# Full-height instead of half-height products with the low parts of the keys, in forgetting attention

## The chip, the cores and the metric

The kernel runs on one core of a Trainium2 chip. The metric is device microseconds from start to end of one execution; the number given for a kernel is the median of several executions.

## What is computed

Two transformer blocks follow each other on 1,024 tokens of width 1,024, in fp32. The second block holds a sliding-window attention and a *forgetting attention* of 8 heads of width 64. The change touches the latter alone:

```python
s = jnp.einsum('bhqd,bhsd->bhqs', qb, kh).astype(jnp.float32) * scale
s = s + cq[..., None] - c_k[:, :, None, :]
s = jnp.where((k_pos[None, :] <= q_pos[:, None])[None, None], s, -jnp.inf)
probs = jax.nn.softmax(s, axis=-1)
return jnp.einsum('bhqs,bhsd->bhqd', probs.astype(vh.dtype), vh)
```

## The kernel before

TensorE multiplies in fp32r, a form that is less exact than fp32. So every operand is split into a high part (a copy rounded to fp32r, made by ScalarE) and a low part (what is left, subtracted by VectorE or GpSimd), and a product is made of several terms that add up in one PSUM bank. A dense layer (`mm3`, line 160) takes three terms for each of eight 128-row blocks: high by high, low by high, and high by the weights' low part, 24 matmuls of 512 columns for a half of the tokens. `dense` (line 170) runs this for one block of 128 output features and calls `then` with each half's PSUM bank; there are three such banks (`mm=3`, line 34).

Forgetting attention works on pairs of heads, j = 0 to 3. A pair's queries and keys come from one dense layer each.

- `queries` (line 1142) makes, for each head e of the pair, a tile of 128 partitions. The 64 partitions of the head's own place hold the high part of the scaled query, the other 64 hold its low part.
- `keys` (line 1159) makes for each head a tile `kh[e]` in which the key's high part stands twice, in the own 64 partitions and in the other 64 (line 1170, ScalarE). Its low part, `kl`, is subtracted on VectorE (line 1172). The sliding-window attention calls it with `twice` true: two tiles `kl[e]`, each with the low part in both halves of the partitions. Forgetting attention calls it with `twice` false: one tile `kl[0]` for both heads, each head's low part in its own 64 partitions.
- `fox_scores` (line 1261) goes over blocks of 128 queries (i = 0 to 7, two for each g), both heads, and pieces of at most 512 keys. A piece is two matmuls into one PSUM bank, of which the tag `sc` has two. Line 1281 multiplies all 128 partitions of the query tile with `kh[e]`, which gives (high + low) by high. Line 1282 multiplies the 64 partitions with the query's high part by the 64 partitions of `kl[0]`, which gives high by low. VectorE then adds the forgetting bias and takes the row's maximum (line 1289), ScalarE takes the exponential (line 1299), GpSimd divides by the sum (line 1304). `fox_pv` (line 1308) transposes the result on TensorE (line 1320), splits it (`split`, line 144) and multiplies it with the values (line 1327).
- `swa_block` (line 1199), the sliding-window counterpart, has the same two terms with full-height tiles in both matmuls (lines 1210 and 1211).

`run` (line 1335) writes the program in this order: scores of a group g, then the values' product of the group before it, then one dense layer of the output gates as work in between (`filler`). After g = 2 it makes the next pair's queries, keys and bias rows. The last pair (j = 3) has no next pair; its `filler` calls find nothing left, and only the first products of the next stage (`after`) can go between.

In this part of the kernel the order on each engine is not written by hand: the compiler's scheduler orders the instructions by a simulated timeline, with the program order as priority. Each engine then runs its own list strictly in that order. The tiles `kh`, `kl`, the bias rows and the values come from a pool with the tag `q`, opened at line 1646 with 10 buffers of 4 KB in each partition.

Of the kernel before, what the change touches and what calls it, by code (L numbers as in the profile page):

```python
# [11 lines left out]
F32R = mybir.dt.float32r  # L12
I32 = mybir.dt.int32
AF = mybir.ActivationFunctionType
ALU = mybir.AluOpType
# [303 lines left out]
def run(thread):  # L319

    while True:
        try:
            next(thread)
        except StopIteration as e:
            return e.value
# [32 lines left out]
def hs(hf):  # L358
    return slice(H * hf, H * hf + H)
# [702 lines left out]
class Attention:  # L1062
# [93 lines left out]
        yield from k.dense(self.w["w_in2"], m, self.xn, then)  # L1156
        return s

    def keys(self, m, twice):

        k = self.k
        nc = k.nc
        kh = [k.q("kh", F32R) for _ in range(2)]
        kl = [k.q("kl", F32R) for _ in range(2 if twice else 1)]

        def then(hf, ps):
            for e in range(2):
                own, other = slice(64 * e, 64 * e + 64), slice(64 - 64 * e, 128 - 64 * e)
                for o in (own, other):
                    nc.scalar.copy(out=kh[e][o, hs(hf)], in_=ps[own])  # L1170
                for o in (own, other) if twice else (own,):
                    nc.vector.tensor_tensor(
                        out=kl[e if twice else 0][o, hs(hf)], in0=ps[own], in1=kh[e][own, hs(hf)], op=ALU.subtract)

        yield from k.dense(self.w["w_in2"], m, self.xn, then)
        return kh, kl
# [84 lines left out]
    def fox_scores(self, st, g):  # L1261
        k = self.k
        nc = k.nc
        qs, kh, kl, cs = st
        out = {}
        for i in (2 * g, 2 * g + 1):

            rest = k.t("S2", tag="tp") if 4 <= i < 6 else None
            for e in range(2):
                own = slice(64 * e, 64 * e + 64)  # L1270
                qc = slice(128 * i, 128 * i + 128)
                diag = k.a("cd", [128, 128])
                nc.vector.tensor_tensor(out=diag, in0=cs[e][:, qc], in1=self.cmsk, op=ALU.add)
                pieces = []
                mx = None
                for c0 in range(0, 128 * i + 128, H):
                    n = min(H, 128 * i + 128 - c0)
                    kc = slice(c0, c0 + n)
                    s = rest[:, 256 * e:256 * e + n] if c0 and rest is not None else k.t("S", tag="tp")[:, :n]
                    ps = k.ps("sc", name="pss")[:, :n]  # L1280
                    nc.tensor.matmul(ps, lhsT=qs[:, e, qc], rhs=kh[e][:, kc], start=True, stop=False)  # L1281
                    nc.tensor.matmul(ps, lhsT=qs[own, e, qc], rhs=kl[0][own, kc], start=False, stop=True)  # L1282
                    d = min(n, 128 * i - c0)
                    parts = [(0, d, cs[e][:, c0:c0 + d])] if d > 0 else []
                    if d < n:
                        parts.append((d, n, diag))
                    for a, b, bias in parts:
                        m2 = self.small()
                        nc.vector.tensor_tensor_reduce(
                            out=s[:, a:b], in0=ps[:, a:b], in1=bias, scale=1.0,  # L1290
                            scalar=NEG if mx is None else mx, op0=ALU.add, op1=ALU.max, accum_out=m2)
                        mx = m2
                    pieces.append(s)
                nm = self.small()
                nc.vector.tensor_scalar(out=nm, in0=mx, scalar1=-1.0, scalar2=None, op0=ALU.mult)
                sums = []
                for s in pieces:
                    sums.append(self.small())
                    nc.scalar.activation(out=s, in_=s, func=AF.Exp, bias=nm, accum_out=sums[-1])
                if len(sums) == 2:  # L1300
                    nc.vector.tensor_tensor(out=sums[0], in0=sums[0], in1=sums[1], op=ALU.add)
                nc.vector.reciprocal(sums[0], sums[0])  # L1302
                for s in pieces:
                    nc.gpsimd.tensor_scalar(out=s, in0=s, scalar1=sums[0], scalar2=None, op0=ALU.mult)  # L1304
                out[i, e] = pieces
        return out
# [28 lines left out]
    def run(self, after):  # L1335
        gates = list(range(16))

        def filler(n=1):
            for _ in range(n):
                if gates:  # L1340
                    run(self.gate(gates.pop(0), (1,)))

        run(self.forget())
        kh, kl = run(self.keys(4, True))
        v = run(self.values(5))
        pend = None
        for kv in range(2):
            bias = self.swa_bias(kv)
            qs = [run(self.queries(2 * kv + b)) for b in range(2)]
            for i in range(8):  # L1350
                sc = self.swa_block(kv, i, qs, kh, kl, v, bias)
                if pend is not None:
                    self.swa_pv(*pend)
                pend = (kv, i, v, *sc)
                if i in GSWA:
                    filler()
        self.swa_pv(*pend)
        pend = None
        q, (kh, kl), cs, v = run(self.queries(6)), run(self.keys(10, False)), self.fox_bias(0), None
        for j in range(4):  # L1360
            nxt = None
            for g in range(4):
                sc = self.fox_scores((q, kh, kl, cs), g)
                if pend is not None:
                    self.fox_pv(*pend)
                if g == 0:
                    v = run(self.values(14 + j))
                pend = (j, v, g, sc)
                if g == 2 and j < 3:
                    nxt = run(self.queries(7 + j)), run(self.keys(11 + j, False)), self.fox_bias(j + 1)  # L1370
                elif (j, g) == (3, 2):
                    filler(16)
                    after = after()
                elif (j, g) == (3, 3):
                    next(after)
                else:
                    filler()
            if nxt is not None:
                q, (kh, kl), cs = nxt
        self.fox_pv(*pend)  # L1380
# [91 lines left out]
def tile_blocks(ctx, tc, a, out):  # L1472
    k = Kernel(ctx, tc, a["vec"])
    nc = k.nc
# [140 lines left out]
    def ffn(ff, x, first, n):  # L1615

        k.a.open("quad", QUAD, "right")
        q = Quads(k)
        q.operands(x)
        run(ff.ups(range(first), x, (1,)))  # L1620
        run(ff.quads(range(first, n), q))
        k.a.close("quad")
        ff.alloc()
        k.a.open("att", ATT, "right")
        for ci in range(len(ff.chunks) - 1):
            run(ff.downs(ci))
# [16 lines left out]
    k.split_engine = nc.gpsimd  # L1643
    ff1.finish(finish1, lambda: att.gates(0, range(16)))
    k.a.close("acc")
    k.a.open("q", dict(q=10))
    br = Branches(k, a, sw_d, fx_d, gt_d, h2_d, h3_d)

    def after():
# [114 lines left out]
```

## Time and profile before

| | before |
|---|---|
| median of 3 runs | 3093.22 us |
| lowest and highest run | 3089.76 and 3104.17 us |
| the profiled execution | 3081.66 us |
| its span, first to last instruction | 3079.9 us |
| mean granted TensorE clock | 0.971 of full speed |

The profile is of one execution, whose time lies 11.56 us under the median. Times inside it are counted from the first instruction. PE is TensorE's matmul, PEld its weight load, DVE is VectorE, ACT is ScalarE, POOL is GpSimd. Forgetting attention runs from about 1778 us to 2115 us, behind the sliding-window attention.

### The profile page before, as it was taken

The page shows a single profiled execution, that of the slowest core. Times are in us where ns is not written, and L with a number is a line of the kernel's source. Part 1 is how long each engine was busy: PE and PEld are TensorE (multiplying, and loading weights), DVE is VectorE, ACT ScalarE, POOL GpSimd, SP SyncE. Part 2 cuts the span into 40 slices and gives each one's busy share as a digit, 9 for nine tenths or more (in the row PEclk, how much of TensorE's full clock was granted, in tenths as well). Part 3 has the DMA queues.
Part 4 walks back from the last instruction along what each step waited for, and adds up shares of the span by engine and source line. Part 5 has one row for each costly group of instructions (what it writes and reads, how often), then busy time and mean ns, then how long its engine had stood idle before and what let it go on. Part 6 is the DMA issues. An engine that isn't in the chain of part 4 may idle for free.

```text
span 3079.9 us, 39432 instructions
## 1 busy us (share of the span) xinstructions
PE 2911.5 (95%) x14392; PEld 2318.3 (75%) x14392; DVE 1813.9 (59%) x3228; ACT 1262.6 (41%) x2187; POOL 1011.8 (33%) x1056
## 2 busy tenths in 40 slices
PE   7969899998998999999999999999998999999997
PEld 5747677777777777788778877777887887888886
DVE  6635555447886666344646755576756444444477
ACT  5434333234544444322445655564334443222233
POOL 2153333421445443003643445550026541000343
PEclk8989899899999999999999999999999999999999
DMA  6533433225422222423542221216533333533224
GB/s 210 183 107 115 117 87 88 76 72 165 153 93 82 82 71 95 150 62 113 175 131 74 83 64 65 66 52 229 178 123 111 122 110 129 186 103 103 89 89 137
DMA packets 188194, 349.72 MB, mean 114 GB/s; under 512 B 58712, under 2 KB 69464, under 8 KB 188000
## 3 DMA queue, kind: packets, MB, share of 16 engines
q1 hardware_dynamic: 146368, 268.51, 28.6%
q10 hardware_dynamic: 41632, 78.69, 7.0%
q8 instruction: 113, 1.85, 0.3%
q14 instruction: 81, 0.66, 0.1%
HBM read 265.05 MB, written 82.08 MB: 113 GB/s over the span
## 4 chain that ended last, share of the span: by engine, by line
PE 62%; DVE 5%; DMA 2%; issue 2%; ACT 1%; POOL 1%; ACTq 0%; DVEq 0%; SPq 0%; POOLq 0%
PE ps_mm L165 38%; PE psX L935 10%; PE psZ L935 5%; PE psY L935 2%; PE pso L1327 1%; PE pss L1282 1%; PE pst L1320 1%; DVE sq L255 1%; PE pss L1281 1%; POOL s L921 1%; PE pso L1243 0%; DVE wl L146 0%; DVE T L907 0%; PE pst L1238 0%; DVE g L1450 0%
## 5 line engine op out<-in xcount | busy, mean ns | idle before, releaser
L145 ACT CAST wh<-wr 128x1024 fp32r<-128x1024 f32 (+2 forms) x343 | 318.2, 928 | 651.8 <-PE ps_mm L165 532.5
L165 PE MATMUL ps_mm<-xh,wh 128*128 128x512 f32 x1344 | 546.5, 407 | 3.5 <-ACT xh L145 1.7
L165 PE MATMUL ps_mm<-xl,wh 128*128 128x512 f32 x1344 | 543.5, 405 | 1.8 <-DVE xl L146 1.8
L146 POOL TENSOR_TENSOR wl<-wr,wh 128x1024 fp32r<-128x1024 f32 (+1 forms) x109 | 257.0, 2359 | 846.5 <-ACT wh L145 663.2
L165 PE MATMUL ps_mm<-xh,wl 128*128 128x512 f32 x1344 | 369.2, 405 | 0.0
L165 PE MATMUL ps_mm<-hh,wh 128*128 128x512 f32 x864 | 342.9, 397 | 7.8 <-DVE acc L1029 4.0
L165 PE MATMUL ps_mm<-hl,wh 128*128 128x512 f32 x864 | 342.6, 397 | 0.0
L146 DVE TENSOR_TENSOR wl<-wr,wh 128x1024 fp32r<-128x1024 f32 (+2 forms) x234 | 251.7, 1076 | 105.2 <-PE ps_mm L165 51.4
L165 PEld LDWEIGHTS ps_mm<-xh,wh 128*128 128x128 f32 x1344 | 256.9, 191 | 61.6 <-issue 3.2
L165 PEld LDWEIGHTS ps_mm<-xl,wh 128*128 128x128 f32 x1344 | 256.9, 191 | 57.4 <-DVE xl L146 2.3
L165 PEld LDWEIGHTS ps_mm<-xh,wl 128*128 128x128 f32 x1344 | 249.7, 191 | 55.2 <-issue 1.9
L1029 DVE TENSOR_TENSOR acc<-acc,ps_mm 128x512 f32<-128x512 f32 x176 | 120.8, 687 | 247.4 <-PE ps_mm L165 239.5
L165 PE MATMUL ps_mm<-hh,wl 128*128 128x512 f32 x864 | 234.1, 397 | 0.0
L165 PEld LDWEIGHTS ps_mm<-hh,wh 128*128 128x128 f32 x864 | 163.7, 189 | 47.3 <-DVE acc L1029 4.4
L677 POOL TENSOR_TENSOR pr<-mt,lt 128x60 f32<-128x60 f32 (+24 forms) x248 | 88.2, 356 | 321.6 <-DMA lt<-d_l 302.8
L165 PEld LDWEIGHTS ps_mm<-hh,wl 128*128 128x128 f32 x864 | 163.7, 190 | 38.2
L165 PEld LDWEIGHTS ps_mm<-hl,wh 128*128 128x128 f32 x864 | 163.8, 190 | 38.0
L921 POOL TENSOR_TENSOR s<-wr 128x512 f32<-128x512 f32 x60 | 88.1, 1468 | 272.4 <-DMA wr<-in_w_up 149.2
L1304 POOL TENSOR_SCALAR S<-S,sm 128x512 f32<-128x512 f32 (+3 forms) x96 | 119.1, 1251 | 94.2 <-DVE sm L1302 65.8
L904 POOL TENSOR_TENSOR r<-xh,xl 128x512 f32<-128x512 f32 x32 | 70.9, 2243 | 227.9 <-PE ps_mm L165 109.6
L255 DVE TENSOR_TENSOR sq<-sq 128x512 f32<-128x512 f32 x112 | 120.8, 1078 | 35.3 <-ACT sq L253 23.1
L805 DVE SCALAR_TENSOR_TENSOR ft<-c,vec,ft 128x1023 f32<-128x1023 f32 x68 | 92.0, 1352 | 40.7 <-ACT ft L803 40.6
(379 smaller groups left out, 5852.3 us busy)
## 6 DMA issues: line engine op xcount, KB each, us to landing
wr<-in_w_in SPq DMA_DIRECT2D x58, 512.0 KB, 4.0
wr<-in_w_up SPq DMA_DIRECT2D x54, 512.0 KB, 3.5
h<-hid SPq DMA_DIRECT2D x108, 256.0 KB, 4.2
wr<-in_w_ff SPq DMA_DIRECT2D x54, 512.0 KB, 3.6
wr<-in_w_in2g SPq DMA_DIRECT2D x32, 512.0 KB, 3.6
hid<-c ACTq DMA_DIRECT2D x26, 512.0 KB, 2.9
wr<-in_w_ff SPq DMA_DIRECT2D x48, 256.0 KB, 2.7
hid<-ft ACTq DMA_DIRECT2D x17, 512.0 KB, 2.6
```

The costliest lines, as they stand in the source:

```text
L145: self.nc.scalar.copy(out=pair[0], in_=src)
L146: (engine or self.nc.vector).tensor_tensor(out=pair[1], in0=src, in1=pair[0], op=ALU.subtract)
L165: self.nc.tensor.matmul(ps, lhsT=a[:, j, :cols], rhs=x[j][hf][part], start=i == 0, stop=i == 3 * kb - 1)
L255: self.nc.vector.tensor_tensor(out=sq, in0=acc, in1=sq, op=ALU.add)
L677: e.tensor_tensor(out=pr, in0=mt[:, :n, i:i + 1].to_broadcast([128, n, m]), in1=lt[:, i:i + 1, i + 1:].to_broadcast([128, n, m]), op=ALU.mult)
L805: nc.vector.scalar_tensor_tensor(out=t[:, i:], in0=src[:, :-i], scalar=c(2 - i), in1=t[:, i:], op0=ALU.mult, op1=ALU.add)
L904: nc.gpsimd.tensor_tensor(out=raw[n], in0=pr[0], in1=pr[1], op=ALU.add)
L921: nc.gpsimd.tensor_tensor(out=o, in0=x, in1=y, op=op)
L935: self.k.nc.tensor.matmul(ps, lhsT=a[:, j], rhs=x[j][part], start=start and i == 0, stop=i == 3 * half - 1, skip_group_check=True)
L1029: k.nc.vector.tensor_tensor(out=o, in0=o, in1=ps, op=ALU.add)
L1281: nc.tensor.matmul(ps, lhsT=qs[:, e, qc], rhs=kh[e][:, kc], start=True, stop=False)
L1304: nc.gpsimd.tensor_scalar(out=s, in0=s, scalar1=sums[0], scalar2=None, op0=ALU.mult)
```

## The change

`keys` always makes two tiles of low parts, each with the low part in both halves of the partitions, as the sliding-window attention had them already. The second matmul of a piece takes all 128 partitions of the query tile and of `kl[e]`, so it gives (high + low) by low, which adds the term low by low. VectorE has two more subtractions in each half of each of the four keys' layers. The pool of tag `q` gets 12 buffers in place of 10.

```diff
-    def keys(self, m, twice):
+    def keys(self, m):
...
         kh = [k.q("kh", F32R) for _ in range(2)]
-        kl = [k.q("kl", F32R) for _ in range(2 if twice else 1)]
+        kl = [k.q("kl", F32R) for _ in range(2)]
...
                 for o in (own, other):
                     nc.scalar.copy(out=kh[e][o, hs(hf)], in_=ps[own])
-                for o in (own, other) if twice else (own,):
+                for o in (own, other):
                     nc.vector.tensor_tensor(
-                        out=kl[e if twice else 0][o, hs(hf)], in0=ps[own], in1=kh[e][own, hs(hf)], op=ALU.subtract)
+                        out=kl[e][o, hs(hf)], in0=ps[own], in1=kh[e][own, hs(hf)], op=ALU.subtract)
...
-                own = slice(64 * e, 64 * e + 64)
...
                     nc.tensor.matmul(ps, lhsT=qs[:, e, qc], rhs=kh[e][:, kc], start=True, stop=False)
-                    nc.tensor.matmul(ps, lhsT=qs[own, e, qc], rhs=kl[0][own, kc], start=False, stop=True)
+                    nc.tensor.matmul(ps, lhsT=qs[:, e, qc], rhs=kl[e][:, kc], start=False, stop=True)
...
-    k.a.open("q", dict(q=10))
+    k.a.open("q", dict(q=12))
```

The calls in `run` lose the second argument of `keys`; nothing else changes there.

## Rows read from the trace of the kernel before

**Rows 1.** The page, busy time of each engine, share of the span, instructions

```profile
PE 2911.5 (95%) x14392; PEld 2318.3 (75%) x14392; DVE 1813.9 (59%) x3228; ACT 1262.6 (41%) x2187; POOL 1011.8 (33%) x1056
```

**Rows 2.** Windows: length, busy PE, PEld, DVE, ACT, POOL, granted clock, DMA

```profile
1648.00:1778.00 130.00, 129.33 (x729) 111.29 (x728) 99.19 (x285) 82.57 (x223) 56.77 (x44) 1.00 0.30 87
...
1778.00:2020.00 242.00, 242.00 (x1167) 185.64 (x1166) 140.51 (x460) 127.86 (x279) 122.17 (x85) 1.00 0.21 64
2020.00:2115.00 95.00, 89.68 (x464) 67.57 (x463) 72.62 (x222) 55.24 (x125) 45.83 (x34) 0.98 0.37 121
```

**Rows 3.** Windows, line 1282 alone: length, busy PE, PEld (instructions), clock, DMA

```profile
1778.00:1850.00 72.00, 8.10 (x19) 3.47 (x19) 1.00 0.21 61
1850.00:1925.00 75.00, 9.07 (x21) 3.84 (x21) 1.00 0.19 64
1925.00:2020.00 95.00, 11.94 (x27) 4.94 (x27) 1.00 0.22 66
2020.00:2080.00 60.00, 13.17 (x29) 5.40 (x29) 0.97 0.17 51
```

**Rows 4.** Waits of VectorE, 1778 to 2020 us: total us, times, longest

```profile
DVE S L1289 <- PE pss L1282: 49.1, 34, 3.0
```

**Rows 5.** Timeline around one piece of 512 keys: start, length, instruction, [idle before]

```profile
1888.40 0.40 PE L165 MATMUL ps_mm<-xl,wh 128*128 128x512 f32 x1
...
1888.64 0.40 PE L165 MATMUL ps_mm<-xh,wl 128*128 128x512 f32 x1
1888.64 0.19 PEld L1281 LDWEIGHTS pss<-kh,qs 128*128 128x128 f32 x1
1888.87 0.39 PE L1281 MATMUL pss<-kh,qs 128*128 128x512 f32 x1
...
1889.19 0.18 PEld L1282 LDWEIGHTS pss<-kl,qs 64*128 64x128 f32 x1 [0.36 <-issue]
1889.19 0.50 PE L1282 MATMUL pss<-kl,qs 64*128 64x512 f32 x1
...
1889.62 0.19 PEld L1327 LDWEIGHTS pso<-pTh,vl 128*128 128x128 f32 x1 [0.24 <-issue]
1889.62 0.39 PE L1327 MATMUL pso<-pTh,vl 128*128 128x256 f32 x1
```

**Rows 6.** Timeline, two pieces in direct succession, 512 and 128 keys

```profile
1893.08 0.40 PE L1281 MATMUL pss<-kh,qs 128*128 128x512 f32 x1
...
1893.40 0.50 PE L1282 MATMUL pss<-kl,qs 64*128 64x512 f32 x1
...
1893.83 0.33 PE L1281 MATMUL pss<-kh,qs 128*128 128x128 f32 x1
...
1894.09 0.32 PE L1282 MATMUL pss<-kl,qs 64*128 64x128 f32 x1
...
1894.35 0.38 PE L1327 MATMUL pso<-pTh,vl 128*128 128x256 f32 x1
```

**Rows 7.** Timeline, sliding-window attention: the same pair of terms, full height, 256 keys

```profile
1736.15 0.28 PE L1210 MATMUL pss<-kh,qs 128*128 128x256 f32 x1
1736.15 0.19 PEld L1211 LDWEIGHTS pss<-kl,qs 128*128 128x128 f32 x1
1736.27 0.28 PE L1211 MATMUL pss<-kl,qs 128*128 128x256 f32 x1
1736.27 0.19 PEld L1210 LDWEIGHTS pss<-kh,qs 128*128 128x128 f32 x1
1736.38 0.28 PE L1210 MATMUL pss<-kh,qs 128*128 128x256 f32 x1
```

**Rows 8.** Instructions on tile kl: count, ns min/median/max, first and last start, forms

```profile
L1282 PE MATMUL pss<-kl,qs x96: 322/490/686, 1778.6 to 2074.1; 64*128 64x512 f32 x48, 64*128 64x128 f32 x16, 64*128 64x256 f32 x16, 64*128 64x384 f32 x16
...
L1172 DVE TENSOR_TENSOR kl<-ps_mm,kh x24: 678/689/696, 1612.3 to 2016.3; 64x512 fp32r<-64x512 f32 x24
```

More of the change, by code (lines that the diff above doesn't have):

```diff
@@ L1343, in run @@
         run(self.forget())
-        kh, kl = run(self.keys(4, True))
+        kh, kl = run(self.keys(4))
         v = run(self.values(5))
@@ L1358, in run @@
         pend = None
-        q, (kh, kl), cs, v = run(self.queries(6)), run(self.keys(10, False)), self.fox_bias(0), None
+        q, (kh, kl), cs, v = run(self.queries(6)), run(self.keys(10)), self.fox_bias(0), None
         for j in range(4):
@@ L1369, in run @@
                 if g == 2 and j < 3:
-                    nxt = run(self.queries(7 + j)), run(self.keys(11 + j, False)), self.fox_bias(j + 1)
+                    nxt = run(self.queries(7 + j)), run(self.keys(11 + j)), self.fox_bias(j + 1)
                 elif (j, g) == (3, 2):
```

## The prediction

> **What bounds the kernel now.** I began with the page: TensorE (PE) is busy 95% of the span, VectorE 59% [rows 1]. That is an average, so I cut the span into stages. In the stretch 1778 to 2020 us, the first three pairs of heads, PE is busy 242.00 us of 242.00 at a granted clock of 1.00, its 2.4 GHz level; VectorE has 58%, ScalarE 53%, GpSimd 50% [rows 2]. The view of waits lists none at all for PE there, while VectorE waits 49.1 us for line 1282's products [rows 4]. So here every microsecond that PE's list becomes shorter should come off the time. In 2020 to 2115 us, the last pair and what follows, PE is busy 89.68 us of 95 and VectorE 76% [rows 2]: PE sometimes runs dry, and time saved on it may turn into waiting.
>
> A busy PE is not a PE at its best pace, since matmuls overlap. What counts is the time from one start to the next. Two dense matmuls of 512 columns start 0.24 us apart, and the next start comes 0.23 us later [rows 5]. A piece of the scores behaves differently. Line 1281 starts at 1888.87, line 1282 at 1889.19, the next matmul at 1889.62: 0.32 and 0.43 us in place of 0.23 twice. The weight loads show why. Line 1281's load starts at 1888.64, while the dense matmul before it streams. Line 1282's load, half height, waits: PEld idles 0.36 us and the load starts together with its own matmul's record, at 1889.19. The next load is full height again and starts only at 1889.62, after 0.24 us of idling [rows 5]. Both changes of height cost; nobody else is waited for ("issue").
>
> The sliding-window attention gives the comparison: the same pair of terms into the same kind of bank, but full height in both. Its load for line 1211 starts at 1736.15, beside line 1210's matmul, and 256-column matmuls start 0.12, 0.11 us apart [rows 7].
>
> **The change part by part.** *The taller matmul.* Time goes by columns, and these stay. The rows of the sliding window are what the changed code will issue, so I expect its pace: 0.23 us for 512 columns, 0.117 for 256. A lone piece of 512 then takes 0.46 us in place of 0.75 and saves 0.29. In direct succession the wide piece takes 0.75 too, and the 128-column piece behind it 0.26 + 0.26 = 0.52 [rows 6]. Two ordinary 128-column matmuls are between 0.12 us (a quarter of 0.46, by columns) and 0.23 (the pace of 256 columns, if the load sets it): it saves 0.29 to 0.40. So a piece saves at least 0.29 us. I take 0.31, because most pieces stand between other work, and 0.34, the mean of 0.29 and 0.40, as upper bound.
>
> There are 96 pieces, 48 of 512, 16 each of 384, 256 and 128 columns [rows 8]. 19 + 21 + 27 = 67 of them start before 2020 us and 29 after [rows 3]. The 67 lie where PE never waits: 67 x 0.31 = 20.8 us, all on the path. The 29 are worth 29 x 0.31 = 9.0 us on PE. Both ends are possible, nothing and all of it; PE is still busy 94% there but leaves 5.3 us idle although no piece was short, so a shorter list will partly end in the wait behind it. What is late next is the chain VectorE (line 1289), ScalarE (1299), GpSimd (1304), then the transposes. I take half, 4.5 us.
>
> *The added subtractions.* `then` runs twice in each of four keys' layers and gets two more operations each time: 16 x 0.689 us = 11.0 us on VectorE [rows 8], all ahead of 2020 us. Cost on the path between 0 and 11.0 us. VectorE rises from 140.5 to 151.5 us in a stretch that shrinks to about 221 us, 68%, still under the 76% at which PE was seen to run dry [rows 2]. The cover is the dense work in PE's list. Queued behind the new operations on VectorE are line 1289's evictions, which free the two score banks, and the probability splits. The new operations also hold the keys' dense bank 1.4 us longer; with three banks of 24 matmuls x 0.23 = 5.5 us each, PE comes back to it 11 us later. I take a fifth, 2.2 us, nearer to nothing since PE shows no wait there.
>
> *The pool.* A pair holds 8 buffers after the change (before 7): two each of kh, kl, bias rows and values. The next pair's keys take 4 (before 3). 8 + 4 = 12 and 7 + 3 = 10, so both fill the pool exactly, and the bias rows wait for a release as now. No DMA is added or moved. In the sliding window two more buffers can hold scores, but PE is busy 129.33 us of 130 there [rows 2], so I give that nothing (at most 0.7 us).
>
> *Sum:* 20.8 + 4.5 - 2.2 = 23.1 us. Against the profiled execution this makes 3081.66 - 23.1 = 3058.6 us. That execution is 11.56 us under the median of the runs, so I carry the difference over: 3093.22 - 23.1 = 3070.1 us.
>
> **The rivals.** *A, VectorE takes over.* The scheduler lays out every engine's list anew, with longer VectorE work at each hand-over of keys. If PE then waits for evictions in half of the 67 pieces, the last 29 give nothing and 2 us of the subtractions show, 10.4 - 2 = 8 us are left: 3085 us. For it: VectorE at 68% is not far from 76%, and new lists can leave PE without dense work in between. Against it: VectorE waits 49.1 us for the very products that come earlier [rows 4].
>
> *B, the change doesn't do what it says:* the pause belongs to something else, say to the second term's load from the same query tile, and stays. Then nothing is saved and the subtractions are hidden: 3093 us. Against it stand the sliding window's pairs, which have all that and no pause [rows 7]. The Trainium skill, "TensorEngine Tiling (Array Packing)", section Key Properties, says that a change of the tiling mode drains TensorE; the two idle times of 0.36 and 0.24 us agree, and the page gives no price.
>
> *C, slower:* a full-height load can't run beside a full-height matmul, and today's half-height load is what is cheap. Its place would be both loads of each of the 96 pieces; its price 0.19 us for each load [rows 5], so a piece of 512 takes 2 x (0.23 + 0.19) = 0.84 us in place of 0.75, 96 x 0.09 = 8.6 us more. With the subtractions partly in the open, by 0 to 11.0 us, the time is 3102 to 3113 us. It decides as soon as loads are no longer started under the matmul before them. The rows speak against it: the 128-row load of line 1281 runs under a 128-row dense matmul, and line 1211's under line 1210's [rows 5, 7]. The Trainium skill, "TensorE: Matmul & The Clock Gate", Part 3, The mechanism, says that a load overlaps with matmuls in flight only where their row groups differ, which would be this rival; the trace disagrees, with the load of 0.19 us at 1736.15 under the 0.28 us matmul of the same rows [rows 7].
>
> **How the numbers follow.** The forecast has 0.70, A 0.18, B 0.07, C 0.05. What a measurement of this kernel can tell from no change is about 0.5%, 15.5 us. The forecast's own span: at the low end all 96 pieces at 0.34, 32.6 us, with 3060.6; two more microseconds for the scatter of the runs, 3058. At its high end 67 x 0.29 = 19.4 us less half of the subtractions, 5.5, is 13.9 us, 3079. The range has to take in A as well, so it goes on to 3086 and leaves out B and C, 0.12, and a little beyond. Faster by over 0.5%: nearly all of the forecast and the better end of A, 0.71. Within 0.5%: most of A, all of B, 0.24. Slower: C, 0.05.
>
> **What would show it.** In the changed profile the loads of lines 1281 and 1282 should start under the matmul before them, without idling, and a lone 512-key piece should take 0.46 us from line 1281's start to the start of the next matmul. Line 1172 has 40 instructions in place of 24, 32 of them in the four pairs. The stretch with the first 67 pieces should be some 19 us shorter, with PE still showing nearly no waits; the last 29 should bring between 0 and 9 us, with more PE waits on lines 1289 and 146. The prediction is wrong if the pace of the pieces stays at 0.75 us (B), if it rises (C), or if PE's waits in the first three pairs come to more than some 10 us (A).

## The result, and the profile after

The changed kernel takes 3063.91 us (median, 3051.18 to 3067.94), beside 3094.70 us of the kernel before in the same series: 30.8 us less, a ratio of 0.9889 with a 95% interval of 0.986 to 0.9918. With more runs (below) it is 0.9904, 0.9889 to 0.992. I had forecast 3070.1 us, 23.1 us less, in a range of 3058 to 3086.

The page of the changed kernel, busy time of each engine, against [rows 1]:

```profile
PE 2883.5 (94%) x14392; PEld 2316.4 (76%) x14392; DVE 1822.0 (59%) x3244; ACT 1260.5 (41%) x2187; POOL 1003.5 (33%) x1056
```

As many matmuls, 28.0 us less of PE, and 16 more operations on VectorE. Line numbers behind 1270 are one lower now: 1280 and 1281 are the two products of a piece.

The timeline of the changed kernel around one piece of 512 keys, against [rows 5]:

```profile
1886.02 0.39 PE L165 MATMUL ps_mm<-xh,wh 128*128 128x512 f32 x1
1886.02 0.19 PEld L1280 LDWEIGHTS pss<-kh,qs 128*128 128x128 f32 x1
1886.25 0.40 PE L1280 MATMUL pss<-kh,qs 128*128 128x512 f32 x1
1886.25 0.19 PEld L1281 LDWEIGHTS pss<-kl,qs 128*128 128x128 f32 x1
1886.48 0.39 PE L1281 MATMUL pss<-kl,qs 128*128 128x512 f32 x1
1886.49 0.19 PEld L165 LDWEIGHTS ps_mm<-xl,wh 128*128 128x128 f32 x1
1886.71 0.40 PE L165 MATMUL ps_mm<-xl,wh 128*128 128x512 f32 x1
```

Every load starts under the matmul ahead of it, none idles first, and the piece takes 0.46 us from line 1280's start to the next matmul's, where it took 0.75.

Now the stages. Windows cut at the first score, the 67th piece and the last product with the values; first the kernel before, then the changed one (length; busy PE, PEld, DVE, ACT, POOL; granted clock; DMA):

```profile
1778.20:2018.00 239.80, 239.80 (x1158) 183.98 (x1156) 139.41 (x455) 127.06 (x277) 121.50 (x84) 1.00 0.21 64
2018.00:2102.80 84.80, 80.02 (x422) 59.91 (x422) 63.99 (x214) 51.03 (x120) 45.17 (x34) 0.98 0.31 100
```

```profile
1789.00:2005.50 216.50, 216.23 (x1159) 183.52 (x1158) 147.82 (x467) 125.65 (x274) 121.95 (x84) 1.00 0.22 69
2005.50:2087.00 81.50, 71.95 (x422) 57.47 (x421) 64.73 (x219) 51.42 (x121) 44.98 (x34) 1.00 0.33 109
```

The stretch of the first 67 pieces is 23.3 us shorter and PE is still busy nearly all of it. VectorE is at 68% there. The last stretch is 3.3 us shorter, PE idles 9.6 us in it in place of 4.8, and VectorE is at 79%. Together 26.6 us. What VectorE waited for the second product fell from the 49.1 us of [rows 4]; this is the changed kernel's view of its waits:

```profile
DVE S L1288 <- PE pss L1281: 24.1, 22, 2.4
```

The two profiled executions, 3081.66 and 3067.94 us, differ by 13.7 us only, because the stages ahead, whose code is the same, took longer in the second. The first product of the sliding-window attention shows it, in the view of the tile pss (count, ns, first and last start), before and after:

```profile
L1210 PE MATMUL pss<-kh,qs x64: 222/281/384, 1648.2 to 1767.3; 128*128 128x256 f32 x56, 128*128 128x128 f32 x8
```

```profile
L1210 PE MATMUL pss<-kh,qs x64: 222/281/383, 1659.2 to 1778.2; 128*128 128x256 f32 x56, 128*128 128x128 f32 x8
```

It starts 11.0 us later. Executions differ by several microseconds there whatever the change (the two profiles of the kernel before have 1648.2 and 1656.5 us), so I read what the change did from stretches that begin behind this point, and from medians.

### The profile page after: what moved, and what is told of

The parts are those of the page before. It is cut to its first block, busy times and chain, and to the rows that moved or that the text cites. A ratio compares the mean times of both kernels' runs of the same rounds, so it can differ in the third digit from the quotient of the medians.

```text
span 3066.2 us, 39452 instructions
## 1 busy us (share of the span) xinstructions
PE 2883.5 (94%) x14392; PEld 2316.4 (76%) x14392; DVE 1822.0 (59%) x3244; ACT 1260.5 (41%) x2187; POOL 1003.5 (33%) x1056
## 4 chain that ended last, share of the span: by engine, by line
PE 59%; DVE 6%; POOL 2%; issue 2%; DMA 2%; ACT 2%; ACTq 0%; SPq 0%; DVEq 0%; POOLq 0%
PE ps_mm L165 39%; PE psX L935 9%; PE psZ L935 5%; PE psY L935 2%; POOL s L921 1%; DVE sq L255 1%; PE pso L1326 1%; PE pst L1319 1%; DMA wr<-in_w_ff 1%; PE pso L1243 0%; PE pss L1280 0%; PE pss L1281 0%; DVE T L907 0%; DVE wl L146 0%; PE pst L1238 0%
## 5 line engine op out<-in xcount | busy, mean ns | idle before, releaser
L677 POOL TENSOR_TENSOR pr<-mt,lt 128x60 f32<-128x60 f32 (+24 forms) x248 | 96.9, 391 | 328.7 <-DMA lt<-d_l 309.9
```

What stands on the lines that cost most here:

```text
L677: e.tensor_tensor(out=pr, in0=mt[:, :n, i:i + 1].to_broadcast([128, n, m]), in1=lt[:, i:i + 1, i + 1:].to_broadcast([128, n, m]), op=ALU.mult)
```

## The experiments

The theory: each change between full and half height makes TensorE pause, the change takes two of them out of each of 96 pieces, and the added subtractions and buffers are hidden. Rivals: the larger pool brings part of the gain; the subtractions cost some of it; the pause belongs to something else than the height.

**The changed kernel again**, without an edit.

> The changed kernel once more, with more runs, to narrow its gain. Its trace shows the stretch from the first score to the last of forgetting attention about 27 us shorter, while the stage ahead of it (unchanged code) was 11 us longer than in the profile of before. If the change does nothing outside this stretch, the ratio settles at 0.990 to 0.992 (25 to 31 us less). If something else in it helps (the larger pool, other lists for the engines), it stays near 0.989 or goes below.

3061.90 us, ratio 0.9904 (0.9889 to 0.992), so 25 to 34 us less. Its profile has 216.40 us for the first 67 pieces and 81.60 for the rest, as the first one had. The ratio came to the place that the stretch alone explains, though its interval also takes in 0.989.

```profile
1781.00:1997.40 216.40, 216.13 (x1158) 183.44 (x1157) 147.75 (x466) 125.50 (x274) 121.68 (x84) 1.00 0.23 69
1997.40:2079.00 81.60, 72.70 (x422) 58.69 (x422) 64.79 (x219) 51.27 (x121) 45.14 (x34) 0.98 0.34 109
```

**The tall product alone.**

```diff
# before
-                    nc.tensor.matmul(ps, lhsT=qs[own, e, qc], rhs=kl[0][own, kc], start=False, stop=True)
+                    nc.tensor.matmul(ps, lhsT=qs[:, e, qc], rhs=kl[0][:, kc], start=False, stop=True)
```

> Only the matmul is made full height: before with line 1282 taking all 128 partitions of the query tile and of the one tile kl[0], no added subtraction, 10 buffers. The second product then adds the low part of the query times the low part of the other head's key in place of its own (that is what it computes differently). Theory (a change of height costs some 0.3 us a piece): all of the gain, 24 to 31 us. Rival (the larger pool brings part of it): 10 us less than the change. Rival (the subtractions cost time on the path): up to 11 us more gain than the change.

3056.37 us, ratio 0.9888 (0.9872 to 0.9904). The whole gain is there with neither the subtractions nor the two buffers. Its median is 5.5 us under the changed kernel's, with intervals that overlap; from the start of the first product of the sliding window to the start of the last product with the values its profile shows 426.2 us, the changed kernel's two profiles 427.6 and 427.7, so about 1.4 us of the difference lie in this part.

**The change without the tall product.**

```diff
# after
-                    nc.tensor.matmul(ps, lhsT=qs[:, e, qc], rhs=kl[e][:, kc], start=False, stop=True)
+                    nc.tensor.matmul(ps, lhsT=qs[64 * e:64 * e + 64, e, qc], rhs=kl[e][64 * e:64 * e + 64, kc], start=False, stop=True)
```

> The change without its matmul: two full tiles kl, 12 buffers, but line 1281 of this kernel multiplies the own 64 partitions alone, so products and results are those of before. Theory: 0 to 3 us slower than before, since 11.0 us more of VectorE lie beside a busy PE. Rival (subtractions on the path): 5 to 11 us slower. Rival (pool brings a gain): some us faster.

3088.94 us, ratio 0.9998 (0.9985 to 1.0011): subtractions and buffers together cost nothing that shows (the interval is about 4 us to either side). This kernel is the best control of all, since its lists of instructions are those of the changed kernel but for two places (a product moved by five dense matmuls on PE, a few neighbours exchanged on VectorE). Its windows, cut at the same instructions:

```profile
1785.60:2025.30 239.70, 239.70 (x1158) 183.73 (x1157) 145.85 (x467) 126.20 (x274) 121.71 (x84) 1.00 0.21 64
2025.30:2114.50 89.20, 85.00 (x422) 63.91 (x423) 63.58 (x218) 51.50 (x121) 45.24 (x34) 0.90 0.31 96
```

The height alone is thus worth 239.7 - 216.5 = 23.2 us in the first 67 pieces, 0.35 us a piece; by medians it is 3088.94 - 3061.90 = 27.0 us. The last stretch differs by 89.2 - 81.5 = 7.7 us, but it has a second difference: the granted clock is 0.90 here and 1.00 in the changed kernel. With the lower level at half speed that is 0.10 x 89.2 x 2, some 18 us at 1.2 GHz.

**The larger pool alone.**

```diff
# before
-    k.a.open("q", dict(q=10))
+    k.a.open("q", dict(q=12))
```

> Before with 12 buffers in place of 10 in the pool of tag q and nothing else. Theory: no difference, within 3 us, since PE is busy without a wait in the stretches that use the pool. Rival (the pool brings part of the gain, by earlier work of the next pair or the next stage): 5 to 10 us faster.

3095.04 us, ratio 1.0012 (0.9998 to 1.0026). No gain from the pool; the interval reaches from 0.6 us less to 8 us more. Its last stretch was the longest of the kernels with the short second product:

```profile
2022.00:2115.70 93.70, 88.18 (x422) 66.30 (x422) 64.16 (x214) 51.13 (x119) 45.04 (x34) 0.87 0.26 80
```

**The kernel before again**, to see whether the buffers and subtractions or the short products let the clock fall.

> The kernel before in one more profiled execution. In its first profile the granted TensorE clock fell to its lower level for 3.4 us in the last pair of heads (from 2041 us), in the kernel with the added subtractions alone for 17.1 us and with the larger pool alone for 24 us, in the changed kernel and the one with tall products alone for 0 to 3.4 us. If short products are what lets the clock fall there, this execution shows a fall of 3 to 25 us between the 67th piece and the last values' product, and a last stretch of 85 to 94 us in place of the 81 us of the changed kernel. If the larger pool or the subtractions caused it, the fall stays at 3.4 us.

One execution: 3097.50 us. Its windows:

```profile
1786.50:2026.30 239.80, 239.80 (x1158) 184.03 (x1156) 139.66 (x455) 126.92 (x277) 121.27 (x84) 1.00 0.21 64
2026.30:2115.00 88.70, 84.18 (x422) 62.64 (x422) 64.37 (x214) 51.25 (x120) 45.04 (x34) 0.92 0.29 96
```

The first stretch is that of the first profile to the tenth of a microsecond. The last is 3.9 us longer than the 84.80 of before, with the clock at 0.92 in place of 0.98. So the kernel before does it too, without added buffers or subtractions, and the first profile, at 0.98, was a mild case.

**Half height in the sliding window.**

```diff
# after
-                nc.tensor.matmul(ps[:, e, :n], lhsT=q, rhs=kl[kv][:, lo:lo + n], start=False, stop=True)
+                nc.tensor.matmul(ps[:, e, :n], lhsT=q[0:64], rhs=kl[kv][0:64, lo:lo + n], start=False, stop=True)
```

> The changed kernel with half-height second products in the sliding-window attention: line 1211 takes 64 of the 128 partitions (the low part of the query of every second head then stands in for its high part in this term, and the term low by low goes). Theory (each change of height has its price, wherever it is): 64 second products, two changes each, about 0.29 us a pair: 18 us slower than the changed kernel, and loads of line 1211 that start only with their own matmul. Rival (the pause belongs to forgetting attention, its score banks or its query tile): no more than 3 us slower, loads still under the matmul before.

3085.52 us, ratio 0.9982 (0.9965 to 0.9999), 23.6 us over the changed kernel where I had expected 18, in another stage, with other tiles and other banks' use. Its timeline (this stretch is all 256 keys), to be held against [rows 7]:

```profile
1737.87 0.38 PE L1211 MATMUL pss<-kl,qs 64*128 64x256 f32 x1
1738.18 0.19 PEld L1210 LDWEIGHTS pss<-kh,qs 128*128 128x128 f32 x1
1738.18 0.38 PE L1210 MATMUL pss<-kh,qs 128*128 128x256 f32 x1
...
1738.49 0.18 PEld L1211 LDWEIGHTS pss<-kl,qs 64*128 64x128 f32 x1
1738.49 0.38 PE L1211 MATMUL pss<-kl,qs 64*128 64x256 f32 x1
1738.80 0.19 PEld L1210 LDWEIGHTS pss<-kh,qs 128*128 128x128 f32 x1
1738.80 0.38 PE L1210 MATMUL pss<-kh,qs 128*128 128x256 f32 x1
...
1739.43 0.50 PE L165 MATMUL ps_mm<-xl,wh 128*128 128x512 f32 x1
...
1739.77 0.39 PE L165 MATMUL ps_mm<-xh,wh 128*128 128x512 f32 x1
```

Starts lie 0.31 us apart where full-height ones lie 0.12 apart, and every load starts with its own matmul. Each change of height costs 0.19 us. The last lines show a part that I had overlooked: the dense matmul behind the last change, at 1739.43, holds the next one up as well, which starts 0.34 us later in place of 0.23. The windows of this stage, here and in the changed kernel's second profile:

```profile
1642.20:1795.00 152.80, 152.80 (x730) 118.62 (x729) 92.01 (x290) 85.51 (x226) 57.96 (x45) 1.00 0.25 74
```

```profile
1650.80:1781.00 130.20, 129.49 (x729) 111.47 (x728) 99.92 (x287) 82.69 (x223) 56.99 (x44) 1.00 0.29 87
```

22.6 us for 64 pairs, 0.35 us a pair, the price of forgetting attention again.

**Both products half height.**

```diff
# before
-                    nc.tensor.matmul(ps, lhsT=qs[:, e, qc], rhs=kh[e][:, kc], start=True, stop=False)
+                    nc.tensor.matmul(ps, lhsT=qs[own, e, qc], rhs=kh[e][own, kc], start=True, stop=False)
```

> Before with both products of a piece half height in forgetting attention (line 1281 takes the own 64 partitions as well, which leaves out the query's low part times the key's high part). Theory (the change of height costs, not the half height): the load of line 1282 now starts under line 1281's matmul and line 1282 follows 0.23 us after line 1281 for 512 keys; the pauses move ahead of line 1281 and behind line 1282, and the time is that of before within some 5 us. Rival (a half-height load always waits): every one of the 192 loads waits, 1281 to 1282 stays at 0.32 us or more, and the time is about 9 us longer than before or more.

One execution: 3083.39 us, and the first 67 pieces take 234.30 us, 5.5 less than before. PE's list there has 109 changes of height, where before has 134: pieces in direct succession now share their two. The timeline of two pieces in succession, 512 and 128 keys:

```profile
1891.72 0.40 PE L165 MATMUL ps_mm<-xh,wl 128*128 128x512 f32 x1
1892.05 0.18 PEld L1281 LDWEIGHTS pss<-kh,qs 64*128 64x128 f32 x1 [0.37 <-issue]
1892.06 0.50 PE L1281 MATMUL pss<-kh,qs 64*128 64x512 f32 x1
1892.16 0.19 PEld L1282 LDWEIGHTS pss<-kl,qs 64*128 64x128 f32 x1
...
1892.39 0.39 PE L1282 MATMUL pss<-kl,qs 64*128 64x512 f32 x1
1892.40 0.18 PEld L1281 LDWEIGHTS pss<-kh,qs 64*128 64x128 f32 x1
1892.62 0.22 PE L1281 MATMUL pss<-kh,qs 64*128 64x128 f32 x1
1892.63 0.19 PEld L1282 LDWEIGHTS pss<-kl,qs 64*128 64x128 f32 x1
1892.68 0.27 PE L1282 MATMUL pss<-kl,qs 64*128 64x128 f32 x1
```

Only the first load waits. The following half-height loads run under half-height matmuls, and 0.23 us separate 1892.39 from 1892.62, the ordinary pace. So the theory holds in this: the change of height costs, not the half height. Two points of my expectation missed: the saving in pieces that follow each other, and the matmul right behind the change, which keeps 0.33 us to the next, not 0.23. About half of the price lies ahead of a change (0.34 us from 1891.72 to 1892.06 in place of 0.23), half behind it.

**The subtraction doubled.**

```diff
# after
-                for o in (own, other):
+                for o in (own, other, other):
                     nc.vector.tensor_tensor(
```

> The changed kernel with the subtraction into the other 64 partitions done twice, with the same result: 16 more operations of 0.69 us on VectorE in forgetting attention (and 4 in the sliding window), so the suspected cost is doubled. The kernel with tall products alone, without these operations, was 5 us faster than the changed kernel, with intervals that touch. If the subtractions cost 5 us on the path, this one is about 5 us slower than the changed kernel; if they lie beside a busy TensorE, it stays within 2 us of it.

3064.28 us, ratio 0.9917 (0.9902 to 0.9931), 2.4 us over the changed kernel by the medians and some 4 by the ratios, with intervals that overlap; that decides nothing between 2 and 5 us. Its stretches do:

```profile
1777.70:1994.50 216.80, 215.58 (x1155) 183.04 (x1155) 155.89 (x476) 124.09 (x272) 121.89 (x84) 1.00 0.23 69
1994.50:2075.80 81.30, 72.18 (x425) 58.38 (x424) 66.19 (x224) 53.01 (x124) 45.17 (x34) 1.00 0.34 110
```

The first 67 pieces have 8.1 us more of VectorE than in the changed kernel and take 0.3 us more, and the last stretch takes 0.2 us less: hidden there, also at 72%. So nothing here puts the 4 us by which the median of the tall product alone was better, beyond the 1.4 us in its profile, down to these operations.

**More dense work for the last pair, less VectorE.** Four attempts to use the idle time of the last pair, all on the changed kernel:

```diff
# after; fill_late, and with (1, 5) fill_later
-GSWA = (1, 3, 5, 7)
+GSWA = (1, 4, 7)
# after; diag_pool; with both edits fill_diag
-                nc.vector.tensor_tensor(out=diag, in0=cs[e][:, qc], in1=self.cmsk, op=ALU.add)
+                nc.gpsimd.tensor_tensor(out=diag, in0=cs[e][:, qc], in1=self.cmsk, op=ALU.add)
```

> The changed kernel with two of the eight gate layers of the sliding window moved behind it: they then run in the last group of the third pair and in the first of the last pair, where TensorE now leaves 10 us of 70 idle. If the last pair is short of dense work, this takes 2 to 8 us off. Rival (the sliding window loses as much, or the last pair is bound by VectorE, busy 83% there): within 2 us of the changed kernel.

> The same with four layers moved. VectorE is busy 77% in the sliding window's stretch of 130 us and would be near 89% of what is left after 4 x 5.6 us of dense work is gone. If TensorE still sets the pace there, another 2 to 5 us off the kernel with two moved; if VectorE takes over in the sliding window, no gain over it or a loss of some us.

> The changed kernel with the masked diagonal bias (64 operations of 128 x 128, 8.0 us of VectorE in the last pair) made on GpSimd. If VectorE's load is what TensorE waits for in the last pair, some 3 to 6 us off. Rival (the chain over GpSimd's division sets the end there, busy 60%): no gain, or slower by the queue ahead of the divisions.

> Both together, two gate layers moved and the diagonal bias on GpSimd. If the two shortages are separate, the gains add up to 5 to 12 us off the changed kernel; if both fill the same idle time, it is the larger of the two.

| | median, us | ratio to before | interval |
|---|---|---|---|
| changed kernel again | 3061.90 | 0.9904 | 0.9889 to 0.992 |
| fill_late | 3064.75 | 0.9906 | 0.9887 to 0.9925 |
| fill_later | 3076.30 | 0.994 | 0.992 to 0.9961 |
| diag_pool | 3064.78 | 0.9912 | 0.9889 to 0.9934 |
| fill_diag | 3068.59 | 0.9916 | 0.9895 to 0.9937 |

None is better, and fill_later is some 11 us worse than fill_late. The windows of the sliding window's stage in fill_late and in fill_later:

```profile
1650.80:1770.30 119.50, 114.50 (x642) 98.23 (x641) 91.13 (x277) 75.41 (x211) 51.46 (x41) 0.97 0.27 80
```

```profile
1656.00:1770.10 114.10, 103.34 (x580) 87.73 (x578) 84.39 (x270) 70.97 (x199) 44.67 (x37) 0.98 0.23 69
```

The dense work that was moved leaves idle time behind: 5.0 and 10.8 us where the changed kernel idles 0.7. The shortage of dense work only moved. Taking load off VectorE alone did not shorten the end either. In diag_pool PE's longest wait there is a dense product of the next stage that waits 4.0 us for ScalarE's split (line 145); what that is worth no run shows, since its lists differ (504 matmuls in the last stretch, in place of 422).

## Why the prediction was right, and where its sizes were off

*What bounds it.* Right. The stretch in which PE had no waits gave all that its list lost, and it kept none of it back: PE is busy 216.23 us of 216.50 there.

*The pace of the tall product.* Right, to the hundredth: 0.23 us for 512 keys, 0.46 a piece.

*The price of a piece.* Too small. I took 0.31 us, 20.8 us for 67 pieces; measured with equal lists it is 23.2 us, 0.35 each. The step that failed is where I stopped the clock: at the start of the matmul behind the piece. That matmul holds up the one behind it by another 0.1 us, as the half-height sliding window shows; in the kernel before itself the matmul behind a 512-key piece among dense ones is followed after 0.34 us, in the changed kernel after 0.23. For a lone wide piece the price is therefore 0.39 us, two changes at 0.19. Piece by piece against the control it is 0.38 us for lone pieces of 512 keys in the mean and 0.29 for those of 128. The narrow pieces, those beside transposes (about 0.34) and two pairs in succession, of which one gained nothing and one half, bring the mean to 0.35; the other pieces in succession cost about what lone ones do.

*The subtractions.* I took 2.2 us; between the control with short products and before there is nothing to see (239.70 and 239.80 us for the first 67 pieces, ratio 0.9998), and doubled beside tall ones they added 0.3 us to the stretch. The cover that I named, dense work in PE's list, was enough, and VectorE rose to the 68% that I had worked out. The agreement of that share is partly luck: I had put 151.5 us in 221, and it was 147.82 in 216.5.

*The pool.* No gain, as forecast.

*The last pair.* I took half of 9.0 us, 4.5. Against the first profile it is 3.3 us, against the second profile of before 88.7 - 81.5 = 7.2, against the control 7.7. At an equal clock, the first profile of before against the second of the changed kernel (both 0.98), it is 84.80 - 81.60 = 3.2 us: PE is busy 7.3 us less there and idles 4.1 us more. So a little less than half of what PE saved reached the end. What the other profiles of the kernel before and the control have beyond that came with a lower clock, which I had not seen; that the short products cause it is likely and not shown (next section but one). If they do, carrying the forecast over from one mild profile to the median left some microseconds out: the gain at the median is larger than the gain seen from that profile.

*The sum.* 23.2 + 7.7 = 30.9 us by the control's profile, 27.0 by the medians of control and change, 26.6 by the first two profiles, for 23.1 forecast. Up to the 26.6, the price of the pieces adds about 2.4 us to the forecast and the subtractions that cost nothing 2.2, and the last pair takes off 1.2.

*The rivals.* A did not come: in the first 67 pieces PE idles 0.3 us in all. It holds in part for the last pair, where PE's idle time doubled. B fell with the kernel that moved the half height to another stage and took the pause along. C fell with the first timeline: full-height loads run under full-height matmuls.

*Left open.* Why the tall product alone is another 5.5 us better by its median, of which its profile shows 1.4: its lists differ from the changed kernel's, since buffers and subtractions differ, and runs of one kernel scatter by as much as that.

## What to carry to other kernels

A product with half the rows and as many columns was not cheaper here than one with all, and among full-height products it cost two changes of height, up to 0.39 us on an engine that otherwise starts a matmul every 0.12 to 0.23 us. Look for weight loads that idle with no one to wait for and start together with their own matmul; then fill the other rows (with a copy, or with a term that is small anyway), or group the half-height products so that they follow each other. Measure a pause up to the second matmul behind it, not the first, and take the price of an engine's pause from a control that has the same lists of instructions.

## What the runs showed of the hardware that I had not expected

In most of these profiles the clock is lower where the height changes. In the stretch from the 67th piece to the last product with the values, where PE runs dry now and then, the granted clock was 0.98, 0.92, 0.90 and 0.87 in the four profiles with the short second product (before twice, subtractions, pool), which, with the lower level at half speed, is 3 to 24 us at 1.2 GHz, and 0.87 with both products short. With the tall product and as much dense work in the stretch it was 1.00, 0.98, 1.00, 1.00 and 0.96 (the changed kernel twice, the tall product alone, the doubled subtraction, and the half-height sliding window). Two of these rows, of the tall product alone and of the kernel with both products short:

```profile
1998.30:2078.70 80.40, 71.04 (x422) 57.31 (x421) 63.61 (x215) 51.13 (x121) 45.17 (x34) 1.00 0.34 111
```

```profile
2013.80:2103.90 90.10, 84.47 (x423) 64.55 (x422) 64.58 (x214) 50.79 (x119) 44.85 (x34) 0.87 0.30 97
```

The busy share of PE does not tell it, 94% in the second, where the clock fell, and 88% in the first, where it did not: the busy time counts pauses and slower matmuls. How much it falls differs from one execution to the next of the same kernel (0.98 and 0.92), and it is part of the scatter of the kernel before. The control with the same lists has 0.90 beside 1.00, in one execution each. But the two groups overlap (0.98 in the first profile of before, 0.98 and 0.96 with the tall product), and with more dense work in the stretch the clock falls with the tall product too, to 0.97 in diag_pool and to 0.94 in fill_late:

```profile
1995.90:2101.20 105.30, 97.55 (x526) 81.54 (x525) 76.70 (x233) 58.24 (x131) 51.22 (x36) 0.94 0.38 122
```

So height is not needed for a fall. That the changes of height make it deeper is likely and not shown, and how it comes about no run here shows.
